# A decoder layer on one core: the last chunk's weights split ahead of the last activations, and two small pads before the feed-forward tiles

## The chip, the core and the metric

The kernel runs on one core of one Trainium2 chip. The metric is the device time of one execution in microseconds (us). A core has TensorE (PE; its weight loads are listed apart as PEld), VectorE (DVE), ScalarE (ACT), GpSimd (POOL) and SyncE (SP), which here only issues transfers. Each engine works through its own list in order, and the lists meet at semaphores: an instruction that waits holds up whatever stands behind it in its own list.

## What is computed

One decoder layer for 256 rows of 1024 values: a norm, one wide projection, two attention mixers, a gated merge, and a feed-forward part with a squared ReLU. The change lies in the feed-forward part alone:

```
x = x + mixed @ w_out[layer]
h2 = rmsnorm(x, norm2_g[layer])
u = jax.nn.relu(h2 @ w_ff1[layer])       # 1024 -> 4096
x = x + (u * u) @ w_ff2[layer]           # 4096 -> 1024
return rmsnorm(x, norm_f_g)
```

## The kernel before

All weights come in 60 chunks of [128, 2048] fp32, in the order of the list CHUNKS, through three buffers `raw`. A product in fp32 is made of three faster ones: every operand is split into a rounded part (suffix h or "hi") and the rest (suffix l or "lo"), and `mm3` issues h x h, h x l and l x h. For weights, `split` does this: ScalarE copies `raw` to `whi` (L111), then VectorE subtracts `whi` from `raw` and writes `wlo` (L113). Both have three buffers.

The feed-forward part begins with chunk 28 (C_FF). Three ff1 chunks come first, then ff2 and ff1 chunks in turn, then ff2 chunks 13, 14 and 15 (numbers 57, 58 and 59). The loop at L952 has one slot per chunk: `run_slot` issues the chunk's matmuls on TensorE and, at positions given as a share of the slot (`at(0.46, ...)`), the other engines' work for later chunks. The positions only set the order of each engine's list; nothing waits for a position as such.

- A ff1 slot (even chunk numbers) has 48 matmuls of 256 columns: `h2h` and `h2l` move, the weights `whi` and `wlo` are stationary. Its output goes through `squares` on ScalarE (L803, L804) into `aq`.
- A ff2 slot for i < 13 has 21 matmuls of 512 columns: seven products of blocks stand in for eight (`seven_mms`). Here the activations are stationary, `ah` and `al` [128, 7 x 128], made from `aq` by `act_parts` (ScalarE L812, VectorE L814, two buffers each), and the weights move: three single blocks of the chunk, split into `sh` and `sl` (L853, L855, two buffers each), and four sums of blocks, made by `sums` into `wt` and split into `whi` and `wlo` (L862, L864).
- Chunks 57 to 59 are multiplied plainly (`ff2_mms`, 24 matmuls of 512 columns per chunk), with whole `whi` and `wlo` moving and the first four columns of blocks of `ah` and `al` stationary. Slot 57 is chunk 57 alone. What comes behind the loop, from L990 on, is one last run: for each of five output pieces the matmuls of chunk 58 and then those of chunk 59, and between them the final norm (`final_a`, `final_b`) and the output.

Three pieces of work of the last slots matter here. In slots 54, 55 and 57 `act_parts` makes `ah` and `al` of blocks 13, 14 and 15. In slot 56 `combine(0)` and `combine(1)`, in slot 57 `combine(2)`, turn the seven sums into outputs: a copy into `fscr` on ScalarE (L893), the rest on VectorE (L889 to L902). And slots 55, 56 and 57 split the weights of chunks 57, 58 and 59 (the branch at L935).

Tiles lie behind one another in SBUF by the order in which they are first asked for. The built program before puts the tiles of the pool "ff" from `ur` on (`ur`, `aq`, `sh`, `sl`, `wt`, `ah`, `al`) at 480 bytes modulo 512 in each partition. `raw`, `whi` and `wlo` lie at 128, `h2h` and `h2l` at 320, the data of `hTh` and `hTl`, which earlier stages use as stationary operands, at 384.

Of the kernel before, what the change touches and what calls it, by code (L numbers as in the profile page):

```python
# [8 lines left out]
F32 = mybir.dt.float32  # L9
# [35 lines left out]
def hybrid_layer(ctx: ExitStack, tc: tile.TileContext, gxd, w, w1c, small, const, gf, out):  # L45
# [16 lines left out]
    def bank(tag, name):  # L62
        return ps.tile([128, 512], F32, name=name, tag=tag)
# [134 lines left out]
    def at(pos, f, *a):  # L198
        ev.append((pos, f, a))

    def run_slot(mms):
        n = len(mms)
        es = sorted(ev, key=lambda e: e[0])
        ev.clear()
        j = 0
        for i, m in enumerate(mms):
            while j < len(es) and es[j][0] <= i / n:
                es[j][1](*es[j][2])
                j += 1
            m()  # L210
        while j < len(es):
            es[j][1](*es[j][2])
            j += 1
# [319 lines left out]
    for sec, c0, n in groups:  # L533
# [6 lines left out]
        for i in range(2):  # L540
            c = c0 + i
# [86 lines left out]
    for g in range(4):  # L628
        accs = [acc_tile(), acc_tile()]
        for i in range(2):  # L630
            c = C_GM + 2 * g + i
# [40 lines left out]
    for sec, c0, kind, evac in (("upn", C_UPN, "n", upn_evac), ("upm", C_UPM, "m", upm_evac)):  # L672
        for i in range(2):
            c = c0 + i
# [26 lines left out]
    def two_blocks(c, ah, al, late=8, whole=None):  # L701

        if late < 8:
            outs = [acc_tile()[:, 0:256] for _ in range(2)]
            whole = None
            order = [range(late), range(late, 8)]
        else:
            whole = whole or acc_tile()
            outs = [whole[:, 0:256], whole[:, 256:512]]
            order = [range(8)]  # L710
        mms = []
        for ks in order:
            for m in range(2):
                mms += wstat(outs[m], c, m * 128, 8, 256, ah, al, ks=ks, last=7)
        return mms, outs, whole
# [3 lines left out]
    FB = {}  # L719

    def open_ff():
        at_stack.close()
        FB["p"] = ctx.enter_context(tc.tile_pool(name="ff", bufs=1))
        FB["o"] = ctx.enter_context(tc.tile_pool(name="ps_o", bufs=1, space=PS))
        p = FB["p"]
        p.tile([128, 96], F32, name="gap")
        FB["h2h"] = p.tile([128, 8, 256], F32R, name="h2h")
        FB["h2l"] = p.tile([128, 8, 256], F32R, name="h2l")
        p.tile([128, 16], F32, name="gap2")
        FB["gfb"] = p.tile([128, 1024], F32, name="gfb")  # L730
        FB["x1"] = p.tile([128, 2, 1024], F32, name="x1")
        FB["scr"] = p.tile([128, 1024], F32, name="fscr")
        FB["fst"] = p.tile([128, 24], F32, name="fst")

    def wout_evac(i, outs, ms=(0, 1)):
        for m in ms:
# [11 lines left out]
    def lo_late(pos, c):  # L748
        for k in range(2):
            at(pos, split, c + 2, k, 2, "l")  # L750
        at(pos + 0.01, load, c + 5)

    def x1_rows(k2s, tiles):
        for k2, tp in zip(k2s, tiles):
            v = tp.rearrange("p (t d) -> p t d", t=2)
            for t in range(2):
                for m in range(2):
                    pe.transpose(v[:, t, m * 128:(m + 1) * 128],
                                 x1T[:, 2 * k2 + m, t * 128:(t + 1) * 128], ident)
            act.activation(FB["x1"][:, :, k2 * 256:(k2 + 1) * 256], v, AF.Copy)  # L760

    for i in range(4):
        c = C_WOUT + i
# [26 lines left out]
    def o_bank(k):  # L790
        return FB["o"].tile([128, 512], F32, name=f"o{k}")
# [15 lines left out]
    def act_parts(i, which):  # L807
        a, b = (1, 8) if i < NSEVEN else (0, 4)
        aq = A[i][0]
        if which == "h":  # L810
            A[i] += [FB["p"].tile([128, 7, 128], F32R, name=n, bufs=2) for n in ("ah", "al")]
            act.activation(A[i][1][:, 0:b - a], aq[:, a:b], AF.Copy)  # L812
        else:
            dve.tensor_tensor(A[i][2][:, 0:b - a], aq[:, a:b], A[i][1][:, 0:b - a].bitcast(F32),  # L814
                              op=ALU.subtract)
# [11 lines left out]
    def seven(c):  # L827
        return c < NCH and CHUNKS[c][0] == "ff2" and CHUNKS[c][1] < NSEVEN
# [42 lines left out]
    def seven_mms(i, c):  # L871
        r = []
        _, ah, al = A[i]
        for name, ka, kb in SEVEN:
            if kb < 3:
                h, l = (x[:, kb * 512:(kb + 1) * 512] for x in singles[c])
            else:
                h, l = (x[c][:, (kb - 3) * 512:(kb - 2) * 512] for x in (hi, lo))
            r += mm3(P[name], ah[:, ka], al[:, ka], h, l, i == 0, i == NSEVEN - 1)
        return r  # L880
# [29 lines left out]
    def ff2_mms(i, c, p):  # L910
        t, c0, n = p
        _, ah, al = A[i]
        r = []
        for k in range(2):
            a = ((1, 0), (2, 3))[k][c0 // 512] * 512 + c0 % 512
            r += mm3(ops[p][:, 0:n], ah[:, 2 * k + t], al[:, 2 * k + t], hi[c][:, a:a + n],
                     lo[c][:, a:a + n],
                     k == 0 and (p == LAST[1] and i == 14 or p == order[1] and i == NSEVEN),
                     k == 1 and i == (13 if p == order[3] else 15))
        return r  # L920

    def slot_events(c):

        if seven(c + 2):
            if c + 2 == C_FF + 3:
                at(0.1, w_singles, c + 2, "h")
                at(0.12, sums, c + 2)
            at(0.15, w_parts, c + 2, "h")
            at(0.2, w_singles, c + 2, "l")
            at(0.3, load, c + 5)  # L930
            at(0.35, w_parts, c + 2, "l")
            if c + 2 > C_FF + 3:
                at(0.4, act_parts, CHUNKS[c + 2][1], "h")
                at(0.6, act_parts, CHUNKS[c + 2][1], "l")
        elif c + 2 < NCH:  # L935
            if c == C_FF + 2:
                at(0.03, act_parts, 0, "h")
                at(0.05, act_parts, 0, "l")
            if seven(c + 3) and c >= C_FF + 2:
                at(0.05, sums, c + 3)  # L940
                at(0.5, w_singles, c + 3, "h")
            for k in range(2):
                at(0.04 + 0.3 * k, split, c + 2, k, 2, "h")
            at(0.46, split, c + 2, 0, 1, "l")
            at(0.51, load, c + 5)
        i = {NCH - 6: 13, NCH - 5: 14}.get(c, 0)
        if i:
            at(0.55, act_parts, i, "h")
            at(0.65, act_parts, i, "l")

    fst, x1, scr = None, None, None
    for c in range(C_FF, NCH - 2):  # L952
        sec, i, _ = CHUNKS[c]
        if c == C_FF:
            lo_late(0.03, c - 1)
        slot_events(c)
        for f, a in prev:
            at(0.02, f, *a)
        prev = []
        if sec == "ff1":  # L960
            if i == 0:
                turn["acc"] = ["acc1", "acc0"]
            elif i == 1:
                turn["acc"] = ["tp"]
            mms, outs, whole = two_blocks(c, FB["h2h"], FB["h2l"], 8 if i else 6)
            turn["acc"] = ["acc0"]
            if i == 1:
                at(0.5, lambda: x1_rows(range(4), [o_bank(k) for k in range(4)]))
            if i == 15:
                at(0.3, combine, 0)  # L970
                at(0.7, combine, 1)
            run_slot(mms)
            prev = [(squares, (i, outs, whole))]
        elif i < NSEVEN:
            if i == 0:
                P.update({n: o_bank(k) for k, n in enumerate("1756")})
                P["2"], P["3"], P["4"] = bank("yb", "yb"), bank("acc1", "acc"), bank("tp", "tp")
            if i == 1:
                at(0.7, rstd2)
            run_slot(seven_mms(i, c))  # L980
        else:
            if i == NSEVEN:
                ops.update({order[0]: P["4"], order[1]: bank("acc0", "acc"), order[2]: P["2"],
                            order[3]: P["3"]})
                at(0.2, combine, 2)
                at(0.3, act_parts, 15, "h")
                at(0.4, act_parts, 15, "l")
            run_slot([m for p in (2, 3, 0, 1) for m in ff2_mms(i, c, order[p])])

    fst, x1, scr = FB["fst"], FB["x1"], FB["scr"]  # L990
# [133 lines left out]
```

## Time and profile before

| | |
|---|---|
| median of 3 executions | 381.5 us (379.88, 381.5 and 381.86) |
| the profiled execution | 381.83 us, its span 380.1 us |
| TensorE busy | 368.2 us, 97% of the span |
| VectorE, ScalarE busy | 312.8 us (82%), 235.6 us (62%) |
| ff1 / ff2 slots in turn | from 223 to 353 us of the span |
| slot 57, last run | from 353 us, from 358 us |

Times in the profile count from the span's start. The span is in 40 slices of 9.5 us below; each digit is the busy share in tenths, PEclk the clock granted to TensorE:

```profile
PE   7999999999999999999999999999999999999883
DVE  3969687897868769856878899999999989998755
ACT  5974455847747567526355978776677666666312
PEclk9999999999999999999999999999999999999988
```

The slices from the 24th to the 36th are the slots in turn, with TensorE and VectorE both over 80% busy; the last three are the end of the last run. Matmuls overlap, so a matmul's listed length (0.39 us, say) is longer than the step from its start to the next one's start; steps are what the slot takes.

### The profile page before, as it was taken

The numbers are of one execution on the slowest core, as the hardware profiler recorded it, in microseconds if no ns is written. First come the engines' busy times: TensorE is split into PE (matmuls) and PEld (weight loads), VectorE is DVE, ScalarE is ACT, GpSimd is POOL, SyncE is SP. The second block draws the span as 40 slices with busy tenths as digits, with TensorE's granted clock in tenths as the row PEclk, the third lists the DMA queues.
The fourth block names the chain that finished last, engine by engine and source line by source line (L and its number), as shares of the span: only waits on it lengthen the run. The fifth ranks groups of instructions, "written<-read, shape, count | busy, mean of one in ns | idle before, by whom it ended". The sixth has DMA issues, their size and how long they took to land.

```text
span 380.1 us, 5982 instructions
## 1 busy us (share of the span) xinstructions
PE 368.2 (97%) x2401; PEld 322.7 (85%) x2401; DVE 312.8 (82%) x459; ACT 235.6 (62%) x368; POOL 3.8 (1%) x14
## 2 busy tenths in 40 slices
PE   7999999999999999999999999999999999999883
PEld 6997888888788887778999999999999999999763
DVE  3969687897868769856878899999999989998755
ACT  5974455847747567526355978776677666666312
POOL 1000000000000000000000000000000000000000
PEclk9999999999999999999999999999999999999988
DMA  7987536333434333541584455545555555554003
GB/s 236 342 340 236 215 111 222 110 112 111 128 135 182 111 112 127 206 160 61 175 325 151 184 178 199 198 192 177 191 201 216 222 222 218 200 185 172 0 2 111
DMA packets 11260, 66.31 MB, mean 174 GB/s; under 512 B 1248, under 2 KB 2784, under 8 KB 3936
## 3 DMA queue, kind: packets, MB, share of 16 engines
q1 hardware_dynamic: 10800, 65.14, 47.2%
q10 hardware_dynamic: 432, 0.79, 0.6%
q8 instruction: 19, 0.31, 0.3%
q14 instruction: 9, 0.07, 0.1%
HBM read 64.87 MB, written 1.05 MB: 173 GB/s over the span
## 4 chain that ended last, share of the span: by engine, by line
PE 89%; DVE 3%; ACT 2%; issue 2%; DMA 1%; SPq 1%; POOLq 0%; POOL 0%; DVEq 0%; ACTq 0%
PE acc L216 58%; PE o L216 10%; PE yb L216 5%; PE tp L216 4%; PE qacc L216 3%; PE kvbacc L216 2%; DVE wlo L113 2%; DMA raw<-in_kva_dram 1%; PE Sa L216 1%; ACT whi L111 1%; PE Sb L216 1%; PE Sb L481 1%; PE Sa L481 1%; PE tp L297 1%; DVE hTl L172 0%
## 5 line engine op out<-in xcount | busy, mean ns | idle before, releaser
L113 DVE TENSOR_TENSOR wlo<-raw,whi 128x1024 fp32r<-128x1024 f32 (+3 forms) x85 | 109.9, 1311 | 13.0 <-ACT whi L111 13.0
L111 ACT ACTIVATE whi<-raw 128x1024 fp32r<-128x1024 f32 (+2 forms) x102 | 95.5, 973 | 38.6 <-PE acc L216 23.1
L216 PE MATMUL acc<-h2h,whi 128*128 128x256 f32 x256 | 71.0, 277 | 0.0
L216 PE MATMUL acc<-h2h,wlo 128*128 128x256 f32 x256 | 71.0, 277 | 0.0
L216 PE MATMUL acc<-h2l,whi 128*128 128x256 f32 x256 | 70.9, 277 | 0.0
L216 PE MATMUL acc<-whi,hTh 128*128 128x512 f32 (+1 forms) x128 | 51.0, 398 | 1.2 <-ACT whi L111 1.0
L216 PE MATMUL acc<-wlo,hTh 128*128 128x512 f32 (+1 forms) x128 | 50.7, 396 | 0.4 <-DVE wlo L113 0.2
L216 PE MATMUL acc<-whi,hTl 128*128 128x512 f32 (+1 forms) x128 | 49.4, 386 | 0.0
L216 PEld LDWEIGHTS acc<-h2h,whi 128*128 128x128 f32 x256 | 48.2, 188 | 0.6
L216 PEld LDWEIGHTS acc<-h2l,whi 128*128 128x128 f32 x256 | 48.1, 188 | 0.5
L216 PEld LDWEIGHTS acc<-h2h,wlo 128*128 128x128 f32 x256 | 48.1, 188 | 0.0
L216 PEld LDWEIGHTS acc<-whi,hTh 128*128 128x128 f32 x128 | 24.2, 189 | 7.4 <-ACT whi L111 1.7
L864 DVE TENSOR_TENSOR wlo<-wt,whi 128x2048 fp32r<-128x2048 f32 x13 | 29.7, 2288 | 0.1
L853 ACT ACTIVATE sh<-raw 128x1536 fp32r<-128x1536 f32 x13 | 19.4, 1489 | 16.0 <-DMA raw<-in_ff_dram 16.0
L216 PEld LDWEIGHTS acc<-wlo,hTh 128*128 128x128 f32 x128 | 24.2, 189 | 5.5 <-DVE wlo L113 1.6
L216 PEld LDWEIGHTS acc<-whi,hTl 128*128 128x128 f32 x128 | 24.1, 189 | 4.3
L862 ACT ACTIVATE whi<-wt 128x2048 fp32r<-128x2048 f32 x13 | 24.8, 1908 | 2.5 <-DVE wt L846 2.5
L855 DVE TENSOR_TENSOR sl<-raw,sh 128x1536 fp32r<-128x1536 f32 x13 | 22.8, 1754 | 0.0
L814 DVE TENSOR_TENSOR al<-aq,ah 128x896 fp32r<-128x896 f32 (+1 forms) x16 | 16.2, 1013 | 4.0 <-ACT ah L812 4.0
L216 PE MATMUL acc<-mxl,whi 128*128 128x256 f32 x64 | 17.8, 278 | 0.2 <-DVE mxl L669 0.2
L216 PE MATMUL acc<-mxh,wlo 128*128 128x256 f32 x64 | 17.9, 279 | 0.0
L216 PE MATMUL acc<-mxh,whi 128*128 128x256 f32 x64 | 17.7, 276 | 0.0
(273 smaller groups left out, 739.7 us busy)
## 6 DMA issues: line engine op xcount, KB each, us to landing
raw<-in_ff_dram SPq DMA_DIRECT2D x32, 1024.0 KB, 5.6
raw<-in_gm_dram SPq DMA_DIRECT2D x8, 1024.0 KB, 4.7
raw<-in_wout_dram SPq DMA_DIRECT2D x4, 1024.0 KB, 4.8
raw<-in_q_dram SPq DMA_DIRECT2D x2, 1024.0 KB, 7.2
raw<-in_qm_dram SPq DMA_DIRECT2D x2, 1024.0 KB, 7.0
raw<-in_km_dram SPq DMA_DIRECT2D x2, 1024.0 KB, 5.0
raw<-in_vm_dram SPq DMA_DIRECT2D x2, 1024.0 KB, 4.7
raw<-in_upn_dram SPq DMA_DIRECT2D x2, 1024.0 KB, 4.7
```

Of the source, the lines that this page charges most:

```text
L111: act.activation(hi[c][:, a:b], raw[c][:, a:b], AF.Copy)
L113: dve.tensor_tensor(lo[c][:, a:b], raw[c][:, a:b], hi[c][:, a:b].bitcast(F32), op=ALU.subtract)
L216: pe.matmul(o, l, r, start=start, stop=stop, skip_group_check=True)
L297: pe.transpose(tp[:, j * 256 + t * 128:j * 256 + t * 128 + 128], src[:, t, (2 * i + j) * 128:(2 * i + j + 1) * 128], ident)
L481: pe.transpose(S[x][:, j, c:c + 128], P[:, 2 * x + j, c:c + 128], ident)
L814: dve.tensor_tensor(A[i][2][:, 0:b - a], aq[:, a:b], A[i][1][:, 0:b - a].bitcast(F32), op=ALU.subtract)
L853: act.activation(singles[c][0], v, AF.Copy)
L855: dve.tensor_tensor(singles[c][1], v, singles[c][0].bitcast(F32), op=ALU.subtract)
L862: act.activation(hi[c], v, AF.Copy)
L864: dve.tensor_tensor(lo[c], v, hi[c].bitcast(F32), op=ALU.subtract)
```

## The change

Three edits:

1. Where a slot splits a chunk whole (L942: ff1 chunks and chunks 57 to 59), ScalarE does it in one instruction of 2048 columns at position 0.05, where it was two of 1024 at 0.04 and 0.34.
2. In slot 57 `act_parts` of block 15 and `combine(2)` move from 0.2, 0.3 and 0.4 to 0.52, 0.52 and 0.53, behind the split of chunk 59 at 0.05 and 0.46.
3. `fst` grows from 24 to 64 columns, and an unused tile of 64 columns ("gap3") is asked for before the first `ah`. In the built program `ur`, `aq`, `sh`, `sl` and `wt` then lie at 128 modulo 512 and `ah` and `al` at 384.

```diff
-        FB["fst"] = p.tile([128, 24], F32, name="fst")
+        FB["fst"] = p.tile([128, 64], F32, name="fst")
@@ act_parts
         if which == "h":
+            if i == 0:
+                FB["p"].tile([128, 64], F32, name="gap3")
             A[i] += [FB["p"].tile([128, 7, 128], F32R, name=n, bufs=2) for n in ("ah", "al")]
@@ slot_events
-            for k in range(2):
-                at(0.04 + 0.3 * k, split, c + 2, k, 2, "h")
+            at(0.05, split, c + 2, 0, 1, "h")
             at(0.46, split, c + 2, 0, 1, "l")
@@ the loop over slots, i == NSEVEN (slot 57)
-                at(0.2, combine, 2)
-                at(0.3, act_parts, 15, "h")
-                at(0.4, act_parts, 15, "l")
+                at(0.52, combine, 2)
+                at(0.52, act_parts, 15, "h")
+                at(0.53, act_parts, 15, "l")
```

ScalarE's list has 274 rows where it had 291; VectorE's, TensorE's and SyncE's keep their lengths, and the order of the matmuls and of the transfers does not change. On ScalarE, from `ah` of block 14 (end of slot 55) to `ah` of block 15 (slot 57), there stood before:

```order
L812 ACTIVATE ah<-aq 128x512 [waits PE_49,Activation_49]
L111 ACTIVATE whi<-raw 128x1024 [waits DMAHW6_49,PE_49]
L893 ACTIVATE fscr<-o_2249 128x512
L111 ACTIVATE whi<-raw 128x1024
L803 ACTIVATE ur<-acc 128x512 [waits PE_49]
L804 ACTIVATE aq<-ur 128x512 [waits DVE_49,Activation_49]
L111 ACTIVATE whi<-raw 128x1024 [waits DMAHW7_49]
L812 ACTIVATE ah<-aq 128x512 [waits PE_49,Activation_49]
L111 ACTIVATE whi<-raw 128x1024
```

and there stands now (line numbers from L812 on are two higher):

```order
L814 ACTIVATE ah<-aq 128x512 [waits PE_49,Activation_49]
L111 ACTIVATE whi<-raw 128x2048 [waits DMAHW6_49,PE_49]
L895 ACTIVATE fscr<-o_2248 128x512
L803 ACTIVATE ur<-acc 128x512 [waits PE_49]
L804 ACTIVATE aq<-ur 128x512 [waits DVE_49,Activation_49]
L111 ACTIVATE whi<-raw 128x2048 [waits DMAHW7_49]
L814 ACTIVATE ah<-aq 128x512 [waits PE_49,Activation_49]
```

The copy into `fscr` has moved behind the whole `whi` of chunk 58, and the whole `whi` of chunk 59 ahead of `ah`. On VectorE, from `wlo` of chunk 58 (slot 56) to the first instruction of the last run, there stood before:

```order
L113 TENSOR_TENSOR wlo<-raw,whi 128x2048 [waits DMAHW6_49,Activation_49]
L897 TENSOR_TENSOR fscr<-fscr,o_2248 128x512 [waits DVE_49]
L889 SCALAR_TENSOR_TENSOR x_1819<-fscr,fst,x_1819 128x512 [waits DVE_49]
L899 TENSOR_TENSOR fscr<-fscr,o_2247 128x512
L889 SCALAR_TENSOR_TENSOR x_1819<-fscr,fst,x_1819 128x512 [waits DVE_49]
L902 TENSOR_TENSOR fscr<-fscr,o_2247 128x512
L889 SCALAR_TENSOR_TENSOR x_1819<-fscr,fst,x_1819 128x512 [waits DVE_49]
L814 TENSOR_TENSOR al<-aq,ah 128x512 [waits PE_49,Activation_49]
L113 TENSOR_TENSOR wlo<-raw,whi 128x2048 [waits DMAHW7_49,Activation_49]
L1027 SCALAR_TENSOR_TENSOR x_1819<-acc,fst,x_1819 128x256
```

and there stands now:

```order
L113 TENSOR_TENSOR wlo<-raw,whi 128x2048 [waits DMAHW6_49]
L899 TENSOR_TENSOR fscr<-fscr,o_2247 128x512 [waits DVE_49]
L891 SCALAR_TENSOR_TENSOR x_1819<-fscr,fst,x_1819 128x512 [waits DVE_49]
L901 TENSOR_TENSOR fscr<-fscr,o_2246 128x512
L891 SCALAR_TENSOR_TENSOR x_1819<-fscr,fst,x_1819 128x512 [waits DVE_49]
L113 TENSOR_TENSOR wlo<-raw,whi 128x2048 [waits DMAHW7_49,PE_49,Activation_49]
L904 TENSOR_TENSOR fscr<-fscr,o_2246 128x512
L891 SCALAR_TENSOR_TENSOR x_1819<-fscr,fst,x_1819 128x512 [waits DVE_49]
L816 TENSOR_TENSOR al<-aq,ah 128x512 [waits PE_49,Activation_49]
L1028 SCALAR_TENSOR_TENSOR x_1819<-acc,fst,x_1819 128x256
```

`wlo` of chunk 59 has moved ahead of the two instructions of `combine(2)` and of `al`; `al` is now the last before the last run.

## The prediction

> **What bounds the kernel now.** I read the page's first part, then the chain of waits from 218 us on, then the tail instruction by instruction.
>
> ```profile
> PE 368.2 (97%) x2401; PEld 322.7 (85%) x2401; DVE 312.8 (82%) x459; ACT 235.6 (62%) x368; POOL 3.8 (1%) x14
> PE 89%; DVE 3%; ACT 2%; issue 2%; DMA 1%; SPq 1%; POOLq 0%; POOL 0%; DVEq 0%; ACTq 0%
> 218.58 2.79 PE o L216 x12
> 221.38 0.68 PE yb L216 x3
> 222.06 0.68 PE acc L216 x3
> 222.74 0.70 PE tp L216 x3
> 223.44 5.47 PE acc L216 x48
> ...
> 352.85 1.40 PE yb L216 x6
> ...
> 358.96 0.96 ACT whi L111
> ...
> 359.94 2.30 DVE wlo L113
> ...
> 362.29 1.43 PE tp L216 x5
> 363.72 4.37 PE acc L216 x12
> ...
> 368.11 0.76 DVE x L1002
> ```
>
> In the chain (start, us, engine and tile) TensorE carries everything from 218 to 358 us: a ff2 slot of 21 matmuls of 512 columns takes 2.79 + 0.68 + 0.68 + 0.70 = 4.85 us, a ff1 slot of 48 matmuls of 256 columns 5.47. So work moved on ScalarE and VectorE there is worth nothing unless it makes TensorE wait, and what a matmul takes is worth all of it, 13 times. At 358 the chain leaves TensorE: ScalarE splits the second half of the last weights (whi), VectorE makes their rest (wlo), and only then TensorE goes on.
>
> ```profile
> 359.71 0.39 PE L216 MATMUL tp<-whi,ah 128*128 128x512 f32 x1
> 362.62 0.40 PE L216 MATMUL tp<-whi,al 128*128 128x512 f32 x1
> 363.56 0.53 PE L216 MATMUL acc<-whi,ah 128*128 128x512 f32 x1
> 367.21 0.40 PE L216 MATMUL acc<-whi,ah 128*128 128x512 f32 x1
> 5.28:8.69 3.41, 2.56 (x12) 1.66 (x10) 1.04 (x2) 1.27 (x3) 0.00 (x0) 1.00 0.98 331
> 360.26:363.68 3.42, 1.39 (x6) 1.17 (x7) 2.37 (x2) 0.00 (x0) 0.00 (x0) 1.00 0.00 0
> 363.68:367.09 3.41, 3.41 (x10) 2.66 (x9) 1.59 (x3) 0.72 (x2) 0.00 (x0) 0.50 0.00 0
> 367.09:370.50 3.41, 3.41 (x16) 2.72 (x16) 1.60 (x3) 0.72 (x2) 0.55 (x1) 1.00 0.02 5
> ```
>
> The windows (stretch, length, busy us of PE, PEld, DVE, ACT, POOL, then the granted clock) show a second loss behind the wait. In 360.26 to 363.68 TensorE was busy 1.39 of 3.42 us; in the next 3.41 us the granted clock is 0.50, then 1.00 again. From 363.56 to 367.21 nine matmuls take 3.65 us; at 1.40 / 6 = 0.233 each they take 2.10. The stall thus costs 362.29 - 359.94 = 2.35 us by itself (359.94 is 359.71 + 0.23) and 1.55 us of half clock afterwards.
>
> **The change: the tail.** The split of the last chunk is one ScalarE instruction at 0.05 of its slot and the last activations (ah) come at 0.52, so ScalarE no longer has half of the weights queued behind an instruction that waits.
>
> ```profile
> 347.24 0.63 ACT L812 ACTIVATE ah<-aq 128x512 fp32r<-128x512 f32 x1 [1.52 <-PE tp L216]
> 347.78 1.04 ACT L111 ACTIVATE whi<-raw 128x1024 fp32r<-128x1024 f32 x1
> 348.73 0.58 ACT L893 ACTIVATE fscr<-o 128x512 f32<-128x512 f32 x1
> 349.20 1.05 ACT L111 ACTIVATE whi<-raw 128x1024 fp32r<-128x1024 f32 x1
> ...
> 354.06 1.04 ACT L111 ACTIVATE whi<-raw 128x1024 fp32r<-128x1024 f32 x1
> 358.33 0.63 ACT L812 ACTIVATE ah<-aq 128x512 fp32r<-128x512 f32 x1 [3.23 <-PE acc L216]
> ...
> 349.34 0.69 DVE L895 TENSOR_TENSOR fscr<-o,fscr 128x512 f32<-128x512 f32 x1
> 350.29 2.29 DVE L113 TENSOR_TENSOR wlo<-raw,whi 128x2048 fp32r<-128x2048 f32 x1 [0.25 <-ACT whi L111]
> 354.59 0.75 DVE L889 SCALAR_TENSOR_TENSOR x<-fscr,fst,x 128x512 f32<-128x512 f32 x1
> 355.26 0.68 DVE L902 TENSOR_TENSOR fscr<-fscr,o 128x512 f32<-128x512 f32 x1
> 358.99 0.69 DVE L814 TENSOR_TENSOR al<-aq,ah 128x512 fp32r<-128x512 f32 x1 [2.26 <-ACT ah L812]
> L862 ACT ACTIVATE whi<-wt 128x2048 fp32r<-128x2048 f32 x13 | 24.8, 1908 | 2.5 <-DVE wt L846 2.5
> ...
> L216 PEld LDWEIGHTS o<-whi,al 128*128 128x128 f32 x43 | 8.1, 188 | 1.7
> ```
>
> These are ScalarE and VectorE in order of time. At 358.33 ah had waited 3.23 us: its buffer is the one of block 13 (two buffers), which TensorE reads until the slot's end. That wait stays; what stands behind it goes. A split of 2048 elements takes 1.91 us (L862 has the same shape). An instruction on these two engines starts some 0.08 us before the one ahead of it ends (354.59 + 0.75 against 355.26), or 0.03 after what it waits for. The replay, with this execution's times:
>
> 1. Slot 56: whi of chunk 58 in one piece, 347.78 to 349.69. The copy into fscr, which stood between the halves, starts 0.1 before that ends (as now) and is done at 350.17; VectorE's L895 follows at 350.20 instead of 349.34, wlo of 58 at 350.20 + 0.69 - 0.08 = 350.8 instead of 350.29: it waits for nothing else. So VectorE is 0.5 us late, and the last update in the slot starts at 355.1 (now 354.59), the next VectorE instruction at 355.8.
> 2. Slot 57: whi of 59, 354.06 to 355.97; wlo of 59, 356.0 to 358.3 (now 362.23). The combination's last two instructions now stand behind it, at 358.2 and 358.9, and al behind those: 359.6 to 360.3. This is the new wait: what queues behind al on VectorE has time until TensorE's group tp is done, but TensorE's third matmul with the last activations needs al.
> 3. TensorE: six matmuls of chunk 58 to 359.71; those with ah and whi, ah and wlo at 359.71 and 359.94 wait for nothing now; the third is due at 360.17 and starts at 360.34. It now starts at 362.62, so 2.28 us go. Bounds: 2.0 (al's weight load of 0.188 not hidden, and 0.1 more on VectorE) to 2.45 (no wait).
> 4. A stall of 0.2 us leaves a window of 3.41 us idle by 6%. In 5.28 to 8.69 TensorE was idle by 25% and the next stretches kept 1.00. So the half clock goes too: 1.55 us.
>
> What follows 368.11 is a fixed sequence of 12.0 us to the span's end; it hangs on the acc group's last matmul and moves as a block. The tail gives 2.28 + 1.55 = **3.83 us**. Merging the split elsewhere in the stage is covered: ScalarE is busy 62%, VectorE's wlo there stands behind other VectorE work, the loads keep their place on SP's queue. Uncovered, a merged split would be 0.9 us late.
>
> On the clock the Trainium skill, "TensorE: Matmul & The Clock Gate", section "Why this matters for your kernels", asks only that gaps stay under about 3 us. Here one of 2.19 us was followed by a clock of 0.50, so the measurement decides; by the page the 1.55 us would come from elsewhere and might stay.
>
> **The change: the pads.** The single blocks (sh, sl, with wt and aq) move from 480 to 128 modulo 512, the activations (ah, al) from 480 to 384. No work is added. The trace has both kinds of pair, moving operand and stationary:
>
> ```profile
> 114.82 0.40 PE L216 MATMUL acc<-wlo,hTh 128*128 128x512 f32 x1
> 117.13 0.39 PE L216 MATMUL acc<-whi,hTl 128*128 128x512 f32 x1
> 122.12 0.39 PE L216 MATMUL acc<-whi,hTh 128*128 128x512 f32 x1
> ...
> 210.10 8.48 PE acc L216 x72
> ...
> 320.10 1.08 DVE L814 TENSOR_TENSOR al<-aq,ah 128x896 fp32r<-128x896 f32 x1
> 321.71 0.39 PE L216 MATMUL o<-sh,ah 128*128 128x512 f32 x1
> ```
>
> whi at 128 against hT at 384 is the pair that the change makes. After a break its first ten steps take (117.13 - 114.82) / 10 = 0.231 us, the next 22 take 4.99 / 22 = 0.227. whi at 128 against ah at 480 never gets there: 0.2325 (2.79 / 12) and 0.233 in the ff2 slots and the tail. sh at 480 against ah at 480 (yb and acc, 0.68 / 3) is at 0.227 already. If all settle, a ff2 slot saves 12 x 0.0055 + 3 x 0.006 = 0.085, in 13 slots 1.1 us; if each slot has ten steps at 0.231 first, 4.85 - (10 x 0.231 + 11 x 0.227) = 0.04, 0.5 us. I take 0.8, and 0.1 for the 16 matmuls between al and the end of the acc group; what slot 57 gains, al's wait takes back. At most ff1's settling comes on top (5.47 against 48 x 0.1135): 0.3. Sum of the pads 0.9, from 0 to 1.5; below zero, ff1 matmuls at 8.48 / 72 = 0.118 as at 210 us would cost 13 x 48 x 0.004 = 2.5 us.
>
> VectorE allows it, just: in the tightest slot al is done at 321.18 and due at 321.71 + 0.46 = 322.17, 0.99 us of slack, of which ten faster slots use 0.6.
>
> **Sum.** The profiled execution took 381.83 us (span 380.1 and 1.7 around it), 0.3 above the median of 381.5. 381.83 - 3.83 - 0.9 = **377.1**. The lowest run shown, 379.88, is nearly one half-clock stretch below the highest; whether it lacked it can't be told.
>
> **Rivals.**
> - The pads do nothing: 381.83 - 3.83 = 378.0. Against it stand the 0.227 and 0.233 of one shape at one clock; for it, that a break precedes every ff2 slot. The Trainium skill, same page, section "Step-by-step: what each phase is for", says this: loading the next weights takes no SBUF read bandwidth from the running matmul, so offsets should not matter.
> - al comes later than I replay and the half clock stays. It needs a window idle by more than 25%, a stall over 0.85 us; VectorE would have to lose 0.7 more. Then 381.83 - (2.28 - 0.8) - 0.9 = 379.4.
> - The half clock isn't the stall's: 381.83 - 2.28 - 0.9 = 378.6.
> - The pads unsettle ff1: 378.0 + 2.5 = 380.5, no measurable change.
> - Slower: the new offsets put every matmul of the 13 slot pairs on its slow step. The place is steady TensorE work, where nothing hides it. The tail's 3.83 us are used up at 0.295 us per pair, 4.3 ns on each of 69 matmuls. With ff1 at 0.118 (0.19 a pair) and the 512-column ones up from 0.231 to 0.240 (0.19) it is 0.38, 4.9 us: 382.9.
>
> **Chances.** Forecast 0.55, pads nothing 0.22, al late 0.07, half clock from elsewhere 0.05, ff1 unsettled 0.07, slower mechanism 0.04. The forecast's own range is 376.2 to 377.8. The range reaches to the late al, 379.4, and down to 375.6: all settled, no wait for al (376.2), and the 0.3 by which this execution lies above the median, with as much for spread. A difference of 0.5% (379.6 and 383.4) is about what can be told from none: faster 0.89, within 0.08, slower 0.03.
>
> **What would show it.** Right: no TensorE gap over 0.5 us near 360, the clock at 1.00 throughout until the matmuls end, wlo of the last chunk ending before al, ff2 slots under 4.82 us by their chain rows, ff1 at 5.47 or less. Wrong: a gap before the matmul with al over 0.85 us, a stretch at 0.50, whi,ah steps still at 0.233, or ff1 slots at 5.6.

## The result, and the profile after

| | before | after |
|---|---|---|
| median of 7 executions each | 381.5 us | 378.72 us (378.34 to 379.16) |
| ratio of the two, 95% interval | | 0.9932 (0.9913 to 0.9952) |
| profiled execution, its span | 381.83, 380.1 us | 379.04, 377.3 us |
| ff2 slot, ff1 slot, both | 4.85, 5.47, 10.33 us | 4.76, 5.65, 10.41 us |

The kernel became 2.8 us faster by the medians, where 4.4 were forecast. The time lies in the range, and the gain is smaller than the forecast. Two executions of the later runs, one of the pads alone and one of before beside the last experiment, took 526 us at a granted clock of 0.66, and every median and ratio below leaves them out. The first line of the page after, and its row of the clock:

```profile
PE 367.8 (97%) x2401; PEld 324.7 (86%) x2401; DVE 312.7 (83%) x459; ACT 234.2 (62%) x351; POOL 3.8 (1%) x14
PEclk9999999999999999999999999999999999999999
```

TensorE is busy as long as before (367.8 against 368.2 us). That says nothing against the tail, since a stall isn't busy time; but half clock is, and 1.55 us of it are gone. So something has been added. The chain of waits (start, us, engine and tile) shows where:

```profile
218.75 2.76 PE o L216 x12
...
229.21 2.72 PE o L216 x12
231.93 0.68 PE yb L216 x3
232.61 0.68 PE acc L216 x3
233.29 0.68 PE tp L216 x3
233.97 5.65 PE acc L216 x48
...
365.60 0.76 DVE x L1003
```

The ff2 slot is 2.72 + 3 x 0.68 = 4.76 us: every 512-column matmul takes 0.227 (slot 0 alone, with 2.76 in its first group, took 4.80). The ff1 slot is 5.65, where it was 5.47: 0.1177 a matmul. A pair costs 0.09 us more than before, and from ff2 slot 0 to ff2 slot 12, twelve pairs, it takes 125.00 us against 123.94, by the first matmul of each. At the end the acc group is done at 365.60, where it was 368.11. The tail by windows (length, busy us of PE, PEld, DVE, ACT, POOL, then the granted clock):

```profile
360.26:363.68 3.42, 3.20 (x15) 2.32 (x14) 2.49 (x5) 0.02 (x1) 0.00 (x0) 1.00 0.00 0
363.68:367.09 3.41, 3.41 (x17) 2.83 (x16) 2.27 (x4) 1.41 (x4) 0.00 (x0) 1.00 0.02 5
```

In the first only 0.22 of 3.42 us are idle, and the next stretch, which had the clock at 0.50 before, has 1.00. What TensorE still waits for is al (timeline of VectorE and TensorE):

```profile
357.31 2.29 DVE L113 TENSOR_TENSOR wlo<-raw,whi 128x2048 fp32r<-128x2048 f32 x1 [0.31 <-ACT whi L111]
359.52 0.68 DVE L904 TENSOR_TENSOR fscr<-fscr,o 128x512 f32<-128x512 f32 x1
360.23 0.75 DVE L891 SCALAR_TENSOR_TENSOR x<-fscr,fst,x 128x512 f32<-128x512 f32 x1
360.90 0.69 DVE L816 TENSOR_TENSOR al<-aq,ah 128x512 fp32r<-128x512 f32 x1
361.03 0.39 PE L216 MATMUL tp<-wlo,ah 128*128 128x512 f32 x1
361.64 0.50 PE L216 MATMUL tp<-whi,al 128*128 128x512 f32 x1 [0.22 <-DVE al L816]
361.98 0.40 PE L216 MATMUL tp<-whi,ah 128*128 128x512 f32 x1
```

wlo of the last chunk ends at 359.60, ahead of the combination's rest and of al, as the replay had it. From the matmul at 361.03 to the next are 0.61 us where a step is 0.227: a stall of 0.38 (the 0.22 in the row count from the listed end of the matmul ahead). The step behind it takes 0.34, another 0.11.

### The profile page after: what moved, and what is told of

Read it like the earlier page. It is cut to its first block, busy times and chain, and to the rows that moved or that the text cites. A ratio compares the mean times of both kernels' runs of the same rounds, so it can differ in the third digit from the quotient of the medians.

```text
span 377.3 us, 5964 instructions
## 1 busy us (share of the span) xinstructions
PE 367.8 (97%) x2401; PEld 324.7 (86%) x2401; DVE 312.7 (83%) x459; ACT 234.2 (62%) x351; POOL 3.8 (1%) x14
## 4 chain that ended last, share of the span: by engine, by line
PE 86%; DVE 5%; ACT 3%; issue 2%; DMA 1%; SPq 1%; POOLq 0%; POOL 0%; DVEq 0%; ACTq 0%
PE acc L216 56%; PE o L216 9%; PE yb L216 5%; PE tp L216 4%; PE qacc L216 3%; DVE wlo L113 3%; PE kvbacc L216 2%; ACT whi L111 2%; DMA raw<-in_kva_dram 1%; PE Sa L216 1%; PE Sb L216 1%; PE Sa L481 1%; PE Sb L481 1%; PE tp L297 1%; DVE hTl L172 0%
## 5 line engine op out<-in xcount | busy, mean ns | idle before, releaser
L113 DVE TENSOR_TENSOR wlo<-raw,whi 128x1024 fp32r<-128x1024 f32 (+3 forms) x85 | 109.9, 1311 | 14.7 <-ACT whi L111 14.7
L111 ACT ACTIVATE whi<-raw 128x1024 fp32r<-128x1024 f32 (+3 forms) x85 | 93.8, 1131 | 41.0 <-PE acc L216 23.1
L216 PE MATMUL acc<-h2h,whi 128*128 128x256 f32 x256 | 71.9, 281 | 0.0
L216 PE MATMUL acc<-h2h,wlo 128*128 128x256 f32 x256 | 71.8, 281 | 0.0
L216 PE MATMUL acc<-h2l,whi 128*128 128x256 f32 x256 | 71.8, 281 | 0.0
L216 PEld LDWEIGHTS acc<-h2h,wlo 128*128 128x128 f32 x256 | 48.9, 191 | 0.0
L803 ACT ACTIVATE ur<-acc 128x512 f32<-128x512 f32 x15 | 9.0, 599 | 19.3 <-PE acc L216 19.3
```

The costliest lines, as they stand in the source:

```text
L111: act.activation(hi[c][:, a:b], raw[c][:, a:b], AF.Copy)
L113: dve.tensor_tensor(lo[c][:, a:b], raw[c][:, a:b], hi[c][:, a:b].bitcast(F32), op=ALU.subtract)
L216: pe.matmul(o, l, r, start=start, stop=stop, skip_group_check=True)
L803: act.activation(r.rearrange("p a q -> p (a q)"), whole, AF.Relu)
```

## Experiments

Two things were open. Does the tail's gain come from the split, and only from it? And what made ff1 slower? **Theory A** says the pads: they settle the 512-column matmuls and, by where the operands start or by how the ff2 slot's last group (tp) leaves TensorE, unsettle the 256-column ones. **Rival B** says the split in one piece: VectorE and ScalarE now work beside other matmuls of the ff1 slots, and TensorE is slowed there. In the tables "starts" are those of sh (with wt), ah and h2h in a partition, in bytes modulo 256, by the built program; 224 and 128 are the 480, 128 and 384 modulo 512 of the text above. A row of matmuls is called settled when its step has come down to the smallest that its width shows, 0.227 us for 512 columns and 0.1134 for 256. A run of one execution is read by its trace, not by its time: slot 0 begins anywhere between 217.6 and 220.4 us.

### One part alone: tail and pads

The change without both pads (the edit is against the change, as in all runs but e2):

```diff
-        FB["fst"] = p.tile([128, 64], F32, name="fst")
+        FB["fst"] = p.tile([128, 24], F32, name="fst")
-            if i == 0:
-                FB["p"].tile([128, 64], F32, name="gap3")
```

> The changed kernel without both pads: merged splits and moved tail alone, offsets as before (480 and 480). Theory A (the pads slow the ff1 slots: the offsets decide in what rhythm a ff1 slot is entered): ff1 slots go back from 5.65 to 5.47 us, ff2 slots from 4.76 to 4.85, a pair of slots from 10.41 to 10.33; no half clock; time 1.0 to 1.2 us under the changed kernel, about 377.6, and 3.7 to 3.9 us under the kernel before. Rival B (the merged split of 2048 columns on ScalarE, which runs in just these slots, slows them): ff1 slots stay at 5.65 us, ff2 at 4.85, time about 379.9.

The kernel before with both pads and nothing else (the edit is against before):

```diff
-        FB["fst"] = p.tile([128, 24], F32, name="fst")
+        FB["fst"] = p.tile([128, 64], F32, name="fst")
+            if i == 0:
+                FB["p"].tile([128, 64], F32, name="gap3")
```

> The kernel before with both pads and nothing else. Theory A: ff2 slots 4.76 us, ff1 slots 5.65, a pair 10.41 against 10.33; the stall of 2.2 to 2.35 us before the matmul with the last wlo and a stretch at clock 0.50 stay; time 0.8 to 1.2 us above the kernel before. Rival B: ff1 slots 5.47, a pair 10.24, time 1 us under the kernel before.

| | median | ratio to before (95%) | ff2 | ff1 |
|---|---|---|---|---|
| tail alone | 378.15 us (10 runs) | 0.9915 (0.9892 to 0.9939) | 4.85 | 5.48 |
| pads alone | 381.96 us (9 runs) | 1.002 (0.9992 to 1.0048) | 4.76 | 5.65 |
| before, beside them | 381.43 us (19 runs) | | | |

The tail alone came out 0.55 us above its expected 377.6. The pads alone were expected 0.8 to 1.2 us above before; measured are 0.5, which the interval does not tell from none. Their traces say more. The tail alone, by the chain, the timeline and the windows:

```profile
224.93 5.25 PE acc L216 x46
```

```profile
254.14 0.39 PE L216 MATMUL acc<-sh,ah 128*128 128x512 f32 x1
254.82 0.40 PE L216 MATMUL tp<-whi,ah 128*128 128x512 f32 x1
255.52 0.28 PE L216 MATMUL acc<-h2h,whi 128*128 128x256 f32 x1
```

```profile
358.40:361.80 3.40, 3.40 (x16) 2.48 (x14) 3.36 (x5) 0.63 (x1) 0.00 (x0) 1.00 0.00 0
361.80:365.20 3.40, 3.40 (x15) 2.71 (x15) 2.05 (x5) 0.72 (x2) 0.00 (x0) 1.00 0.00 0
```

With the split in one piece and the old starts, ff1 runs at 5.25 / 46 = 0.114 us, as before; whi,ah keeps its 0.233 (0.70 / 3) and sh,ah its 0.227 (0.68 / 3). Twelve of the thirteen ff1 slots take 5.48; in one, at 327.8 us, TensorE waited for wlo of VectorE and the slot took 5.82. Rival B falls. The clock is 1.00 in the tail without the pads, so these have no part in that. The pads alone, by the chain and the windows:

```profile
316.30 5.65 PE acc L216 x48
...
362.47 1.43 PE tp L216 x5
```

```profile
360.40:363.81 3.41, 1.34 (x6) 1.13 (x7) 2.41 (x2) 0.00 (x0) 0.00 (x0) 1.00 0.00 0
363.81:367.22 3.41, 3.41 (x10) 2.63 (x9) 1.60 (x3) 0.72 (x2) 0.00 (x0) 0.50 0.00 0
```

Here the split is the old one, and ff1 takes 5.65. The stall is back (359.83 to 362.47 between two matmuls), and the half clock with it. So the tail comes from the edits 1 and 2 together, and ff1's loss from the pads: both shown, each by a run that has it alone. The two edits of the tail were not run apart.

### Which pad, and which starts

One pad each, then pads of other sizes that move only sh and its neighbours, only ah, or h2h:

```diff
 e3: no "gap3"          e4: fst 24 columns
 e5: gap3 24 columns    e6: fst 24 columns, gap3 40 columns
 e7: gap 112, gap2 64   e8: gap 80, gap2 32 (columns; 96 and 16 in the change)
```

> The changed kernel with the first pad alone: single blocks and activations both at 128 modulo 512. Theory A, if what counts is the distance of moving and stationary start: distance 0, as sh on ah had before at 480 on 480, so ff2 slots 4.76 us; the ff1 pace is open: 5.47 if the entry happens to fit, 5.65 if not, and one of the two in all 13 slots. Rival B: ff1 5.65.

> The changed kernel with the second pad alone: single blocks at 480, activations at 224 modulo 512. Theory A: whi on ah has distance 416, sh on ah 256; the sh blocks at 0.227, the whi blocks between 0.227 and 0.240, a ff2 slot 4.76 to 4.90 us; ff1 at 5.47 or 5.65 in all 13 slots. Rival B: ff1 5.65.

> The changed kernel with the second pad cut to 24 columns: single blocks at 128, activations at 224 modulo 256. Kernels whose activations differ by 256 alone had the same steps, so starts are told modulo 256: sh 128, ah 224, whi 128, h2 64. Theory A (equal starts of moving and stationary settle at 0.227, unequal ones don't; the way a ff2 slot is left decides which of two paces the next ff1 slot has): all ff2 matmuls unequal, 0.231 to 0.240 each, a ff2 slot 4.87 to 4.90 us; as tp, the last group, is unsettled as before, ff1 stays at 5.47. Rival C (it is the single blocks' start that slows ff1, since the ff1 slot is followed by them): ff1 at 5.65.

> The changed kernel without the first pad and with the second cut to 40 columns: single blocks at 480 (224 modulo 256), activations at 128. Theory A: whi on ah equal, so the o groups from the second on and tp settled at 0.227; sh on ah unequal, up to 0.240; a ff2 slot 4.78 to 4.85 us; tp settled, so ff1 at 5.65. Rival C: ff1 at 5.47.

> The changed kernel with h2h and h2l moved by 64 bytes, from 64 to 128 modulo 256, everything else at the same place modulo 256. Theory A with 'equal starts settle' for every width: ff1 at 5.45 us in all slots, ff2 at 4.76, a pair 10.21. Against it: in the changed kernel the last 256-column pieces, with equal starts, took 0.120 a step; by that ff1 would be at 48 x 0.120 = 5.76.

> The same with h2h and h2l at 0 modulo 256, a distance of 128 from whi. Theory A says nothing of this distance: ff1 between 5.44 (0.1134 a step) and 5.76 (0.120). If ff1 stays at exactly 5.65, the start of h2 doesn't matter and theory A's starts are the wrong measure.

| | starts: sh, ah, h2h | ff2 | ff1 | time of the one run |
|---|---|---|---|---|
| before | 224, 224, 64 | 4.85 | 5.47 | 381.83 |
| after | 128, 128, 64 | 4.76 | 5.65 | 379.04 |
| e3: fst alone | 128, 128, 64 | 4.76 | 5.65 | 379.74 |
| e4: gap3 alone | 224, 224, 64 | 4.85 | 5.48 | 378.08 |
| e5: sh alone | 128, 224, 64 | 4.91 | 5.65 | 381.7 |
| e6: ah alone | 224, 128, 64 | 4.88 | 5.46 | 377.8 |
| e7: h2 at 128 | 128, 128, 128 | 4.79 | 5.75 | 381.3 |
| e8: h2 at 0 | 128, 128, 0 | 4.81 | 5.75 | 382.68 |

In e4 ah lies at 224 modulo 512, in before at 480, and nothing differs; in e3 it lies at 128, in after at 384, and nothing differs. So gap3 does nothing beside the larger fst, and the starts matter modulo 256. Two rows of the chain each tell the rest, e5 first:

```profile
255.30 0.70 PE tp L216 x3
256.01 5.65 PE acc L216 x48
```

```profile
264.01 0.70 PE tp L216 x3
264.71 5.46 PE acc L216 x48
```

In both (the second is e6) the group tp runs unsettled, 0.70 for three, and the ff1 slot behind it takes 5.65 in one and 5.46 in the other. So the part of theory A by which tp's own pace decides ff1's falls. Its part on equal starts holds only by half: in e6 tp's operands both start at 128, and theory A had them settled and the slot at 4.78 to 4.85, yet tp took 0.70 and the slot 4.88. Settled rows of 512 columns were seen only with equal starts, but equal starts don't ensure it. What goes along with 5.65 in every row so far is the start of sh and its neighbours at 128: **rival C**. It is odd, though, for no ff1 matmul reads one of them: h2h, h2l, whi and wlo lie where they lay. And e7 shows that the rule of equal starts doesn't hold for ff1's matmuls: with h2h at 128 like whi theory A had 5.45, and they are slower still, 0.120. With h2h at 0 (e8) it is 0.120 too.

### One break in each slot

If the same operands at the same starts can run at 0.1134 and at 0.1177, then it isn't the starts alone that set the pace: there are two rhythms, and what comes ahead of a row of matmuls picks one (**theory D**). The slots of before point that way:

```profile
305.89 0.28 PE L216 MATMUL acc<-h2h,whi 128*128 128x256 f32 x1
...
306.48 0.28 PE L216 MATMUL acc<-h2h,wlo 128*128 128x256 f32 x1
...
307.84 0.28 PE L216 MATMUL acc<-h2h,wlo 128*128 128x256 f32 x1
```

The first five steps of this ff1 slot take 0.118 on the mean (0.59 / 5), the next twelve 0.113 (1.36 / 12), and so on to its end. In the change all 48 take 0.118. So what before has and the change lacks is the passage from one pace to the other. By C nothing in the ff1 slot itself could change its pace. In e9 the fourth matmul of each ff1 slot of the thirteen pairs is cut into two of 128 columns, in e10 the last one of each ff2 slot into two of 256; the change is otherwise whole, and what is computed the same.

```diff
+            if i >= 3:
+                def cut(o=outs[0], w=hi[c][:, 256:384]):
+                    for s in (slice(0, 128), slice(128, 256)):
+                        mm(o[:, s], w, FB["h2h"][:, 1, s], False, False)
+                mms[3] = cut
```

> The changed kernel with one matmul near the start of each ff1 slot (the fourth) cut into two of 128 columns: same result, one break in the rhythm. Theory D (the same operands have two rhythms, 0.1134 and 0.1178 a step, the slot's entry picks one, and a break can move TensorE from one to the other): the steps behind the cut go to 0.113, the 44 left save 0.19 us against the cost of the cut itself of about 0.1, a ff1 slot 5.55 to 5.6 us. Rival C (the single blocks' new start slows ff1 by itself): the steps stay at 0.118, a ff1 slot 5.75.

```diff
+        def cut(al=al, ka=ka, h=h):
+            for s in (slice(0, 256), slice(256, 512)):
+                mm(P["4"][:, s], al[:, ka], h[:, s], False, i == NSEVEN - 1)
+        r[-1] = cut
```

> The changed kernel with the last matmul of each ff2 slot cut into two of 256 columns: the break stands ahead of the ff1 slot. Theory D: the entry is another, ff1 at 5.45 to 5.5 us if it is the fast one, a pair 10.23 to 10.28; at 5.65 the entry was the same. Rival C: ff1 5.65, a pair 10.43.

The timeline of e9 at a slot's start, and the chain of e10:

```profile
254.21 0.28 PE L216 MATMUL acc<-h2h,wlo 128*128 128x256 f32 x1
254.33 0.33 PE L216 MATMUL acc<-h2h,whi 128*128 128x128 f32 x2
254.50 0.33 PE L216 MATMUL acc<-h2l,whi 128*128 128x256 f32 x1
254.67 0.28 PE L216 MATMUL acc<-h2h,wlo 128*128 128x256 f32 x1
...
256.03 0.28 PE L216 MATMUL acc<-h2h,wlo 128*128 128x256 f32 x1
```

```profile
254.73 0.69 PE tp L216 x4
255.42 5.46 PE acc L216 x48
```

In e9 the steps ahead of the cut are 0.118 us. The two halves and the matmul behind them take 0.34 (254.33 to 254.67) where two whole ones take 0.24; then twelve steps take 256.03 - 254.67 = 1.36, 0.113 each, and the slot's rest keeps that. The slot takes 5.57: the cut costs 0.1, and the rhythm that it brings gives 0.19 back. In e10 the cut costs 0.01 (tp 0.69) and the ff1 slot behind it takes 5.46. Same operands, same starts, either pace: that there are two is shown, and that a cut ahead can move TensorE from the slow one to the fast one; C can at most say which is entered. The ff2 slots take 4.78, 0.02 more than in the change, so a pair is 10.24 where the change has 10.41 and before 10.33. One ff1 slot of e10, the twelfth, stayed at 0.118 and took 5.67, so the cut does not ensure the fast pace.

### The wait for al, and both together

In e11 the split of block 15's activations stays at 0.52 and 0.53 and the combination goes behind it:

```diff
-                at(0.52, combine, 2)
+                at(0.54, combine, 2)
```

> The changed kernel with combine(2) behind the last activations: al stands right behind the last wlo on VectorE. If al queued behind combine(2) is what TensorE waits for in the last run (a step of 0.61 us at 361.03 instead of 0.23), the step is 0.23 here and the end comes 0.3 to 0.4 us earlier from there on. Rival (the wait is for the last wlo itself): the step stays at 0.6.

```profile
361.28 0.39 PE L216 MATMUL tp<-whi,al 128*128 128x512 f32 x1
```

The matmul ahead of this one started at 361.05 and the next one at 361.50: no wait for al. The group takes 12 x 0.227 = 2.72 us here and 3.23 in the change, so the wait cost 0.51 in all, more than the 0.3 to 0.4 expected: 0.38 ahead of the matmul with al and 0.13 in the steps behind it. e12 has the edits of e10 and e11:

> The changed kernel with the cut of the last matmul of each ff2 slot and with combine(2) behind the last activations. Theory D with the queue on VectorE: a pair of slots 10.26 us against 10.41 in the changed kernel (1.8 us over twelve), no wait before the matmul with al (0.4 us), no half clock before the matmuls end: about 376.6, 1.2% under the kernel before and 0.5% under the changed one. Rival C: as the changed kernel, 378.3 to 378.7.

It took 376.55 us (median of 4, 376.28 to 376.7) against 381.77 for before beside it (6 runs): 0.987 (0.9832 to 0.9908). Its chain, and one row of VectorE:

```profile
259.35 2.73 PE o L216 x12
262.08 0.68 PE yb L216 x3
262.76 0.68 PE acc L216 x3
263.44 0.69 PE tp L216 x4
264.13 5.46 PE acc L216 x48
...
335.81 5.87 PE acc L216 x48
...
357.35 2.72 PE tp L216 x12
360.07 2.73 PE acc L216 x12
...
362.83 0.76 DVE x L1008
```

```profile
333.65 2.28 DVE L113 TENSOR_TENSOR wlo<-raw,whi 128x2048 fp32r<-128x2048 f32 x1
```

TensorE is on the chain into the tail's two groups, each 12 x 0.227. So this version beats before, and its four executions lie below all seven of the change, though the two were not taken beside each other. One slot of the thirteen did not gain: at 335.81 it takes 5.87, since its third matmul waits for this wlo (to 335.93), and all its steps from the fourth on are 0.118. So a break can also leave a slot on the slow pace. From the change's profiled execution to this one the pairs give 1.88 us by their first and last matmuls (0.17 in most, 0.24 lost in the late one), al 0.51, and a slot 0 that began 0.40 earlier the rest; the two took 379.04 and 376.28. Expected were 1.8 and 0.4.

That late wlo shows the next limit. VectorE's own round for a pair, from one wlo of L113 to the next with no wait in it, is 10.22 us at the shortest in before (314.03 to 324.25), and TensorE's pair is now 10.24. One late transfer (VectorE waited 0.65 us for raw at 330.5) is then enough to hold TensorE up.

## Why the prediction was right, and where it was not

**The number.** 378.72 us lies in the range only because that was stretched up to the price of a late al, 379.4, which did not happen; it lies outside the forecast's own 376.2 to 377.8, and nearer than to 377.1 to the times of two rivals that did not happen either (pads do nothing, 378.0; half clock from elsewhere, 378.6). So the time alone decides nothing, and that it fell in the range is in part luck. By the signs that the prediction set, all those of being right hold but one, and that one is a sign of being wrong: ff1 slots at 5.65.

**The tail: right.** From the start of slot 57 to the end of the acc group are 15.22 us before and 11.39 after: 3.83, the forecast's own sum, where 0.1 of the pads was to come on top. To the start of the third matmul with al 2.30 of it are gained, where 2.28 were forecast, and behind it 1.53, where the half clock was sized at 1.55. The order of the replay held at each step, and the half clock comes and goes with the stall: gone without it (e1), there with it (e2). The Trainium skill, "TensorE: Matmul & The Clock Gate", section "Why this matters for your kernels", asks only that gaps stay under about 3 us, and by that the 1.55 us could have stayed. The runs decide against it: a gap of 2.2 us had half clock behind it in before and in e2. The rivals on the tail (al late by 0.7 us, half clock from elsewhere) are refuted by the windows.

**The wait for al: right in kind, 0.2 us too small.** Forecast was a stall of 0.17, measured 0.38. VectorE came as replayed: the matmul that waits began 7.64 us after slot 57's first matmul, where 7.65 were forecast (360.34, with slot 57 from 352.69). TensorE came 0.23 earlier: slot 57 became 0.17 shorter (5.61 to 5.44), as the text said that al's wait takes back what slot 57 gains, and the eight matmuls ahead of the wait 0.06.

**The pads on ff2: right, sized low.** "If all settle" was priced at 1.1 us, and 0.8 was taken. All did, but for slot 0's first group: the thirteen slots gave 1.14 us. One reading behind the price was off: three of the twelve matmuls in o are sh on ah, with equal starts, and in before they weren't settled either (0.229 to 0.236 in the slot at 249.4 us), so the offsets were not the only thing that kept that group slow. The Trainium skill says on the same page, "TensorE: Matmul & The Clock Gate", section "Step-by-step: what each phase is for", that loading the next weights takes no read bandwidth from the running matmul. That offsets should not matter was concluded from it by the prediction, for a rival; the conclusion falls, with 4.85 and 4.76 for the same matmuls at other starts.

**The pads on ff1: wrong.** The step that failed is "at most ff1's settling comes on top": it allowed ff1 a gain of up to 0.3 us and let a loss stand only as a rival with 7 chances in 100. ff1 lost 0.18 us in 13 slots, 2.3 us, where that rival was priced at 2.5 by the 0.118 of the matmuls at 210 us. That rival had the mechanism for ff1; its time of 380.5 left out what ff2 gained. No reason is given there for the "at most". If it was that ff1's own operands don't move, e9 and e10 show that this is no protection: those operands have two rhythms, and what runs ahead has a part in which one is taken. The 0.118 had been in the trace of before beside the 0.114, at 210 us and in the first five steps of each ff1 slot, and should have been read as two states that a row of matmuls can be in, not as the price of an unlikely case.

**VectorE's slack: misread, at no cost here.** The prediction looked at al alone and found 0.99 us. The tightest instruction was wlo of the ff1 chunk (L113): in before one slot already waited for it (316.21 us, 0.02 us longer), and in e1 and e12 one slot each took 0.34 and 0.41 longer by it. In the change none did, with its longer pairs.

**The sum.** By the first and last matmuls of the slots the profiled executions differ like this: slot 0 began 0.17 us later; thirteen ff2 slots gave 1.14, thirteen ff1 slots took 2.29, slot 57 gave 0.17, the tail from there to VectorE's row on the acc group 3.66 (9.81 to 6.15), and what lies behind it 0.28 (11.94 us before, 11.66 after). That is 2.79 us, and the spans differ by 2.79 (380.05 and 377.26). Against the forecast the ff1 slots are the one large term that is missing; ff2's, sized 0.3 low, and the 0.28 behind the tail, where a fixed sequence was forecast, made up for a part. The pads cost 1.15 us net in the slots' rows, and 1.0 with slot 57. By time they can't be told from no change (378.15 without them and 378.72 with, 381.43 and 381.96 on the old tail).

**What stays open.** Why these starts go with these rhythms isn't known: neither how the operands are read nor TensorE's inside is in the trace. Nor is it known which of the tiles that move with sh (sl, wt, aq, ur) decides how ff1 is entered, since they were only moved together, nor why one break leads to the fast pace and another to the slow one. Other starts of the 512-column operands weren't tried, and the 0.28 us behind the tail weren't looked into.

## What to carry to other kernels

A steady row of matmuls has a step of its own, to be read from starts and not from lengths. Where one shape shows two steps in one trace, as 0.118 and 0.113 did here, price a row of that shape at either, also where only its neighbours are touched. When padding moves operands, measure every kind of slot apart: here ff2 gained 1.14 us and ff1 lost 2.29. A cut in one matmul at the seam, at 0.01 us, was worth more here than the pads: 0.17 us a pair. A stall of two microseconds in a row of matmuls should be priced with the stretch at half clock behind it (here 1.55 us on 2.35), and work that TensorE doesn't wait for (here the combination) belongs behind what it waits for. And once TensorE's pair is as short as VectorE's round, the next gain is on VectorE.

## What the runs showed of the hardware

- Steps of matmuls of 512 columns in float32r, the type of the rounded parts: 0.227 us, settled, only in rows whose moving and stationary operand start at the same byte modulo 256 (sh,ah in before; all of them after). With other starts the groups' means are 0.232 to 0.235 (before, e5, e6). Equal starts are not enough: tp in e6 has 0.234 behind rows with unequal ones.
- Steps of 256 columns: 0.1134 or 0.1177 for the same operands, 0.120 with h2h at 0 or 128 (e8, e7). A cut matmul switched 0.1177 to 0.1134 (e9, and e10 in twelve slots of thirteen); in before the passage came after five steps without one; in e12 a slot in which TensorE waited for wlo kept 0.118.
- Two matmuls of 128 columns and the next of 256 took 0.34 us where two whole ones take 0.24 (e9); a matmul of 512 cut into two of 256 cost 0.01 (e10).
- Half clock for 3.41 us followed a gap of some 2.2 us in the tail of before and e2 (windows 59% and 61% idle), and gaps of 1.0 to 1.5 us between 8 and 10 us in e8, e1 and e10 (windows 38, 44 and 49% idle). Early windows idle by 25% (before) and 36% (e3, e4) kept 1.00. There is no sharp limit in idle share: a window at the end of e1 was 46% idle and the next kept 1.00.
- Executions differ by up to 2.8 us in when slot 0 begins (217.6 to 220.4). The three latest (219.7 to 220.4), e1, e8 and e10, are those with that early stretch at half clock, the others have none between 10 and 15 us; these kernels are with and without pads, so it is spread and not the edits'.
